# All score products of two attentions with 128 rows, in a fused kernel of two transformer blocks

## The chip, the cores and the metric

The kernel runs on one core of one Trainium2 chip, in one launch. The metric is its time on the device in microseconds; the median of several runs is given. A profile comes from one execution taken by the hardware profiler. The engines are named as the profile names them: PE (TensorE), PEld (its weight loads), DVE (VectorE), ACT (ScalarE), POOL (GpSimd) and SP (SyncE, which here issues most DMAs).

## The reference

Two blocks of two layers each, on 1024 tokens of 1024 features, all in float32. The first block has a dilated window attention (18 heads of 64 features in three groups with dilations 1, 4 and 16) and a latent attention. Each layer of the second block mixes tokens by a differential attention, a retention and a pooling, and then runs a convolutional MLP. The change concerns the scores of two of them:

```python
# dilated attention, one group: blocks of R queries against 3 R keys
s = jnp.einsum('bdhnqe,bdhnke->bdhnqk', qs, kb).astype(jnp.float32) * (Dh ** -0.5) + bias[:, None]
p = jnp.exp(s - m)
o = jnp.einsum('bdhnqk,bdhnke->bdhnqe', p, vb.astype(jnp.float32)) / denom
# differential attention: 4 heads, two maps m of 64 features each, causal
s = jnp.einsum('bhmqd,bhmkd->bhmqk', q_blk, k).astype(jnp.float32) * scale
p = jax.nn.softmax(jnp.where(mask, s, -jnp.inf), axis=-1)
a = p[:, :, 0] - lam * p[:, :, 1]
```

## The kernel before

A float32 matrix is kept as two float32r parts, a high part (the rounded value) and a low part (what is left), and a product is the sum of high times high, high times low and low times high. For scores over 64 features the kernel puts the high part of q in 64 of the 128 rows of a tile and the low part in the other 64. One product with 128 rows against k's high part, which stands in both halves, then gives (high + low of q) times high of k. A second product adds high of q times low of k; before the change it has 64 rows, because k's low part stands only in the half where q's high part is.

**Differential attention** (`diff_attention`, once per layer of the second block). Query tiles of 128 tokens are taken one after the other, 32 in all (four heads of eight). In step n, `scores(n, m)` computes the scores of both maps of tile n against its t + 1 key tiles (t = n % 8), so with 128 to 1024 columns, in pieces of at most 512, in two PSUM buffers `y`. A third product `dccm` adds the causal mask to the last 128 columns. VectorE takes the row maximum from PSUM (L1551), ScalarE the exponential (L1553), VectorE combines the two maps (L1559). `transpose(n - 2, ..)` and `values(n - 3)` follow two and three steps later, `project(n + 3)` computes q and k three tiles ahead, and `turn(n + 2)` transposes and splits them: k into `dk` (high) and `dkl` (low), tiles of a whole head with two buffers, q into `dq`. PE executes all this in the order of the program (`self.pin`).

**Dilated attention** (in `phase_A`). Nine groups are run through, three dilations g for each of three pairs of heads hp. `dil_batches` gives the score batches of a group; `step` lays the scores of a batch, the transposes and value products of the batch before, and pieces of the projection of the next group (`dil_project`, half projections of 24 products) between each other. The order of PE is the program's; a planner orders the other engines by the costs it assumes. `dil_project` evacuates q and k from PSUM (two buffers `g`) into their parts: `split_q` (L637, L639), `split_k` (L647, L649, L652). Group g = 2 keeps q and k in plain float32 (L631) and computes its scores in one product with 64 rows, which PE executes as two instructions. v goes through `vt` (L664) to be transposed. After the three groups of a head pair, `dil_weights` reads the row statistics back from DRAM, forms the weights of the groups and stores them (L835); `dil_product` loads them as `wb` (L528) and multiplies `sg` by them (L529).

**The raw ring.** `raw()` hands out five buffers of 128x1024 in turn. In the dilated attention weight columns come through it (`load_w`, L217, then split on DVE and POOL, L199 and L203), and the rows of `ada_w` of a background job, `mod_jobs` (L542, L552). SP issues DMAs in order, so one that waits for a buffer holds those behind it.

Of the kernel before, what the change touches and what calls it, by code (L numbers as in the profile page):

```python
# [12 lines left out]
F32 = mybir.dt.float32  # L13
F32R = mybir.dt.float32r
# [83 lines left out]
class UT:  # L98
    """Transposed activations, split in two float32r parts: [feature, token]."""
# [12 lines left out]
class Pools:  # L112
    """Several pools, chosen by tag."""
# [8 lines left out]
class TagPool:  # L122
    """One pool per tag (a new pool waits only for the pools it overlaps); a tile without a tag is a tag of its own."""
# [18 lines left out]
class Kern:  # L142
# [30 lines left out]
    def psum(self, ctx, left="", right=""):  # L173
        """One PSUM pool per tag, stacked from either end."""
        for side, tags in (("left", left), ("right", right)):
            for t in tags:
                self.ps.tags[t] = self.pool(ctx, "ps" + t, space=PSUM, side=side)

    def pp(self, tag, bufs, shape=None):
        """PSUM tile; a tag of a phase always comes with the same bufs."""  # L180
# [5 lines left out]
    def split(self, hi, lo, src, scale=None):  # L186
        """hi = float32r(src), lo = src - hi (src times scale), src in PSUM or SBUF."""
# [8 lines left out]
    def wsplit(self, hi, lo, raw, eng=None, cut=1, act=False):  # L196
        """Split, the high part on ScalarE if act; the low part in as many pieces as cut says (short ones delay other work
        of the engine less)."""
# [9 lines left out]
    def load_w(self, pool, w, c0, n, kts=KT, tag="w", bufs=None, dve=0, cut=1):  # L208
        """Weight columns c0..c0+n, split: w[kt][part] is [128, n]; every dve-th chunk on VectorE alone."""
# [15 lines left out]
    def next_w(self, c0, ahead=0):  # L225
        """The weight columns at c0 of the list in self.order, or those after them."""
# [7 lines left out]
    def gemm_T(self, w, ut, out, cols=slice(0, P)):  # L234
        """out [128 features, 1024 tokens] in PSUM, as two halves."""
# [10 lines left out]
    def gemm_N(self, ps, w, cols, lhs, kts=KT):  # L246
        """ps [128 tokens, features]; lhs(part, kt) is the stationary operand."""
# [7 lines left out]
    def transposes(self, dst, src, n):  # L255
        """dst [.., n, 128] = blocks of src [128, n * 128] transposed."""
# [3 lines left out]
    def to_T(self, src, ut, t):  # L260
        """src [128 tokens, 1024] in SBUF -> ut token tile t."""
# [6 lines left out]
    def rsqrt(self, y, v, pool, src=None, mul=1.0, eps=0.0):  # L268
        """y = v ** -0.5 (integer first guess, three Newton steps), v = src * mul + eps if src is given."""
# [20 lines left out]
    def silu2(self, out, src, tmp):  # L290
        """out = 2 silu(src) = src (1 + tanh(src / 2))."""
# [3 lines left out]
    def rms_rstd(self, src, n, eps, junk, pool):  # L295
        """[128, 1] = (mean(src ** 2) + eps) ** -0.5 over the free axis."""
# [13 lines left out]
    # ---------------------------------------------------------------- setup  # L310
# [11 lines left out]
    def transposed_columns(self, dst, rows_ap, nrow, pool):  # L322
        """dst [128, nrow] = rows_ap [nrow, 128] transposed."""
# [7 lines left out]
    # ---------------------------------------------------------------- first block, layer 0  # L331
    def phase_A(self, x_in):
        nc, i = self.nc, self.i
        with ExitStack() as ctx:
# [6 lines left out]
            with ExitStack() as c0:  # L341
# [23 lines left out]
                # relative position bias vectors, one row per head  # L365
# [11 lines left out]
                # shift and scale, one feature per partition  # L377
# [7 lines left out]
                # column c of block c: ones  # L385
# [69 lines left out]
            def fill(n):  # L455
                """PE work of the projections and gates, as many pieces."""
# [6 lines left out]
            def step(job, n):  # L463
                """The scores of job, with the rest of the one before it."""
# [42 lines left out]
    def dil_gate(self, lp, ut, w_in, hp, g, sgs):  # L507
        """2 silu(gate) of head pair hp of group g, transposed."""
# [13 lines left out]
    def dil_product(self, lp, hp, g, sgs, os, wtd, yT):  # L522
        """y^T rows of head pair hp of group g: attention times weight times gate."""
        nc = self.nc
        sg = sgs[hp, g]
        wb = lp.tile([P, S], F32, tag="wb", bufs=1, name=self.nm("wb"))
# [8 lines left out]
    def mod_jobs(self, lp, cs, jobs):  # L535
        """Thirds of silu(c) @ ada_w + ada_b of a layer, to DRAM, and the convolution taps by channel."""
# [63 lines left out]
    def dil_project(self, lp, ut, w_in, hp, g, res):  # L600
        """q, k, v of heads (2 hp, 2 hp + 1) of group g, tokens in the order of the group; v with tokens on
        partitions."""
# [24 lines left out]
        def tiles(*names):  # L627
            return [lp.tile([P, S], F32 if g == 2 else F32R, tag=n, bufs=2, name=self.nm(n)) for n in names]

        def plain(t, copy):  # L630
# [1287 lines left out]
```

## Time and profile before

| | before |
|---|---|
| median of 3 runs | 4187.02 us (4184.10 to 4189.52) |
| span of the profiled execution | 4168.8 us |
| PE busy | 3945.4 us, 95% |
| PE weight loads busy | 3282.7 us, 79% |
| VectorE busy | 2430.4 us, 58% |
| ScalarE busy | 1371.7 us, 33% |
| dilated attention | 77 to 637 us of the span |
| differential attentions | 1777 to 1993 us and 3077 to 3293 us |

The span runs from the first to the last instruction of the program; no other time of that execution is recorded, and the median of the runs lies 18.2 us above it. Matmuls are pipelined and the profile models their ends, so consecutive ones overlap in the rows; the distance from one start to the next is what a product takes of PE's time. In a row, `y<-dkl,dq 64*128 64x512` means: tile `y` is written from `dkl` (moving) and `dq` (stationary), 64 rows by 128 weight columns, 512 moving columns. What stands in brackets at the end is the idle time of the engine just before, and what ended it.

### The profile page before, as it was taken

How to read it: one execution, taken by the hardware profiler on the slowest of the kernel's cores; microseconds unless marked ns; L12 is line 12 of the kernel's file. 1: busy time of each engine (PE TensorE's matmuls, PEld its weight loads, DVE VectorE, ACT ScalarE, POOL GpSimd, SP SyncE). 2: the span in 40 equal slices, each digit the busy share in tenths (PEclk: the TensorE clock that was granted, in tenths of full speed). 3: DMA queues.
4: the chain of work that ended last, by engine and by line, in shares of the span. 5: the costliest groups of instructions: out<-in, count | busy, mean ns of one | idle time of the engine just before them, and what ended most of it. 6: DMA issues, size and time to landing. Idle time of an engine off the chain costs nothing. (4 is left out here: it accounts for less than half of the span.)

```text
span 4168.8 us, 54321 instructions
## 1 busy us (share of the span) xinstructions
PE 3945.4 (95%) x21085; PEld 3282.7 (79%) x21085; DVE 2430.4 (58%) x4606; ACT 1371.7 (33%) x2908; POOL 1087.9 (26%) x1016
## 2 busy tenths in 40 slices
PE   7989896899999889999999999997999999999998
PEld 5768775788888778988778888886988778888886
DVE  6545445947787767578753434438568764444436
ACT  3323331126777632255421111113235431111111
POOL 1111211410221322233133232324133222222233
PEclk9989998999999999999999999998999999999999
DMA  6363727320110243110421111113111231111112
GB/s 234 90 81 87 90 57 124 112 67 21 38 35 19 79 130 97 46 32 26 137 81 51 45 51 46 46 56 115 46 42 37 82 122 50 46 46 51 41 51 81
DMA packets 318896, 290.79 MB, mean 70 GB/s; under 512 B 70779, under 2 KB 273267, under 8 KB 318638
## 3 DMA queue, kind: packets, MB, share of 16 engines
q1 hardware_dynamic: 313362, 268.23, 23.8%
q10 hardware_dynamic: 5276, 19.08, 1.5%
q8 instruction: 167, 2.74, 0.3%
q14 instruction: 91, 0.75, 0.1%
HBM read 240.26 MB, written 51.72 MB: 70 GB/s over the span
## 5 line engine op out<-in xcount | busy, mean ns | idle before, releaser
L203 POOL TENSOR_TENSOR wl<-wr,wh 128x1024 fp32r<-128x1024 f32 (+1 forms) x253 | 497.9, 1977 | 1553.1 <-DVE wh L199 1458.8
L199 DVE CAST wh<-wr 128x1024 fp32r<-128x1024 f32 x222 | 180.2, 813 | 713.5 <-PE y L151 310.6
L151 PE MATMUL y<-uh_m,wl 128*128 128x512 f32 x1056 | 415.8, 394 | 4.7 <-DVE z L1643 4.2
L151 PE MATMUL y<-uh_m,wh 128*128 128x512 f32 x1056 | 418.6, 396 | 0.0
L151 PE MATMUL y<-ul_m,wh 128*128 128x512 f32 x1056 | 417.6, 395 | 0.0
L1796 ACT ACTIVATE cv<-y,cw 128x1024 f32<-128x1024 f32 x66 | 79.8, 1209 | 775.7 <-PE y L151 775.7
L151 PE MATMUL g<-uh_a,wl 128*128 128x512 f32 x568 | 234.8, 413 | 32.7 <-DVE sg L293 32.6
L151 PEld LDWEIGHTS y<-uh_m,wl 128*128 128x128 f32 x1056 | 198.2, 188 | 54.8 <-issue 4.6
L151 PEld LDWEIGHTS y<-uh_m,wh 128*128 128x128 f32 x1056 | 198.2, 188 | 48.2
L151 PEld LDWEIGHTS y<-ul_m,wh 128*128 128x128 f32 x1056 | 198.2, 188 | 47.5 <-DVE ul_m L191 0.9
L151 PE MATMUL g<-ul_a,wh 128*128 128x512 f32 x568 | 227.7, 401 | 0.5 <-POOL ul_a L422 0.4
L151 PE MATMUL g<-uh_a,wh 128*128 128x512 f32 x568 | 227.0, 400 | 0.0
L151 PE MATMUL y<-wo,yh 128*128 128x512 f32 x784 | 217.5, 400 | 2.7 <-ACT yh L1168 2.5
L191 DVE TENSOR_TENSOR pt<-t,pt 128x512 fp32r<-128x512 f32 x256 | 165.8, 680 | 21.9 <-ACT pt L190 21.0
L151 PEld LDWEIGHTS y<-wo,yh 128*128 128x128 f32 x784 | 147.7, 191 | 36.4 <-ACT yh L1168 4.3
L151 PE MATMUL y<-wl,hh 128*128 128x512 f32 x440 | 175.2, 398 | 0.0
L151 PE MATMUL y<-wh,hh 128*128 128x512 f32 x440 | 174.9, 398 | 0.0
L151 PE MATMUL y<-wh,hl 128*128 128x512 f32 x440 | 174.8, 397 | 0.0
L1005 DVE TENSOR_REDUCE nm<-s 128x1 f32<-128x1024 f32 x128 | 155.7, 1216 | 27.4 <-PE s L151 26.7
L151 PE MATMUL g<-wl,uh_n 128*128 128x256 f32 x576 | 166.2, 289 | 2.9 <-DVE dv L191 2.4
L151 PE MATMUL g<-wl,uh_f 128*128 128x256 f32 x576 | 166.0, 288 | 3.0 <-DVE dv L191 2.5
L151 PE MATMUL v<-pt,v 128*64 128x256 f32 (+1 forms) x1024 | 154.9, 294 | 10.2 <-DVE o L1040 10.2
(450 smaller groups left out, 10263.1 us busy)
## 6 DMA issues: line engine op xcount, KB each, us to landing
wr<-w_up SPq DMA_DIRECT2D x88, 512.0 KB
wr<-ada_w SPq DMA_DIRECT2D x48, 512.0 KB
wr<-w_down SPq DMA_DIRECT2D x44, 512.0 KB
wr<-a_w_in SPq DMA_DIRECT2D x36, 512.0 KB
wr<-w_in SPq DMA_DIRECT2D x24, 512.0 KB
xs<-wr SPq DMA_DIRECT2D x16, 512.0 KB
wr<-xs ACTq DMA_DIRECT2D x16, 512.0 KB
wr<-w_in SPq DMA_DIRECT2D x32, 256.0 KB
```

Source lines behind the costliest of these rows:

```text
L151: ins = self.nc.tensor.matmul(*args, **kw)
L191: nc.vector.tensor_tensor(lo, src, hi.bitcast(F32), OP.subtract)
L199: (self.nc.scalar.copy if act else self.nc.vector.tensor_copy)(hi, raw)
L203: (eng or self.nc.gpsimd).tensor_tensor(lo[..., cs], raw[..., cs], hi[..., cs].bitcast(F32), OP.subtract)
L1005: nc.vector.tensor_reduce(nm, sp, AX.X, OP.max, negate=True)
L1796: nc.scalar.activation(t, ps, AF.Identity, bias=cw[:, 3, c:c + 1], scale=cw[:, 2, c:c + 1])
```

## The change

The low part of k is written to both halves of the rows, so that the second score product can use all 128 rows of q as well: it gives (high + low of q) times low of k. This holds for the differential attention and for all three groups of the dilated one; group 2 loses its plain float32 path and gets the same two float32r products as the others. In the differential attention `dk` and `dkl` become tiles of 512 keys with three buffers, and one subtract of both maps replaces two. In the dilated attention `split_k` subtracts four times instead of two, into two tiles `kl0` and `kl1`. To make room, `vt`, `wb` and the tile of the statistics are taken from the raw ring instead of having buffers of their own. Docstrings and comments are removed throughout, which the diff below leaves out.

```diff
@@ dil_product, dil_weights
-        wb = lp.tile([P, S], F32, tag="wb", bufs=1, name=self.nm("wb"))
+        wb = self.raw()
@@ dil_project
         def tiles(*names):
-            return [lp.tile([P, S], F32 if g == 2 else F32R, tag=n, bufs=2, name=self.nm(n)) for n in names]
-
-        def plain(t, copy):
-            return lambda h, ps: copy(flat(t)[:, :, halves[h]], ps)
+            return [lp.tile([P, S], F32R, tag=n, bufs=2, name=self.nm(n)) for n in names]
...
         def split_k(k, low):
             def evac(h, ps):
                 for r, t in zip(rows, k):
                     nc.scalar.copy(flat(t[r])[:, :, halves[h]], ps[r])
-                for r, t in zip(rows, k):
-                    nc.vector.tensor_tensor(flat(low[r])[:, :, halves[h]], ps[r],
-                                            flat(t[r])[:, :, halves[h]].bitcast(F32), OP.subtract)
+                for r, o, t, u in zip(rows, rows[::-1], k, low):
+                    for d in (r, o):
+                        nc.vector.tensor_tensor(flat(u[d])[:, :, halves[h]], ps[r],
+                                                flat(t[r])[:, :, halves[h]].bitcast(F32), OP.subtract)
                 for r, o, t in zip(rows, rows[::-1], k):
                     nc.scalar.copy(flat(t[o])[:, :, halves[h]], ps[r])
...
-        if g == 2:
-            out += tiles("q0", "k0")
-            evacs = [plain(out[0], nc.scalar.copy), plain(out[1], nc.vector.tensor_copy)]
-        else:
-            q, k, low = tiles("q0", "q1"), tiles("k0", "k1"), tiles("kl")[0]
-            out += [q, (k, low)]
-            evacs = [split_q(q), split_k(k, low)]
-        vt = lp.tile([P, S], F32, tag="vt", bufs=1, name=self.nm("vt"))
+        q, k, low = tiles("q0", "q1"), tiles("k0", "k1"), tiles("kl0", "kl1")
+        out += [q, (k, low)]
+        evacs = [split_q(q), split_k(k, low)]
+        vt = self.raw()
@@ dil_batches, Job.scores
-                    if g == 2:
-                        kern.mm(sp[:rows, j, :], q[rs, q0:q0 + rows], k[rs, k0:k0 + wd], start=True, stop=True)
-                    else:
-                        qa, ka, low = q[hd.a][:, q0:q0 + rows], k[0][hd.a][:, k0:k0 + wd], k[1][rs, k0:k0 + wd]
-                        kern.mm(sp[:rows, j, :], qa, ka, start=True, stop=False)
-                        kern.mm(sp[:rows, j, :], qa[rs], low, start=False, stop=True)
+                    qa = q[hd.a][:, q0:q0 + rows]
+                    for n in range(2):
+                        kern.mm(sp[:rows, j, :], qa, k[n][hd.a][:, k0:k0 + wd], start=(n == 0), stop=(n == 1))
@@ diff_attention, turn
-            if t == 0:
-                ks[h] = (lp.tile([P, 2, S], F32R, tag="dk", bufs=2, name=self.nm("dk")),
-                         lp.tile([P, S], F32R, tag="dkl", bufs=2, name=self.nm("dkl")))
-            kk, kl = ks[h]
+            if t % 4 == 0:
+                ks[h, t // 4] = [lp.tile([P, 2, 512], F32R, tag=x, bufs=3, name=self.nm(x)) for x in ("dk", "dkl")]
+            kk, kl = ks[h, t // 4]
...
-            for m, r in enumerate(rows):
-                nc.vector.tensor_tensor(kl[r, ts], tp[r, 1 + m], kk[r, m, ts].bitcast(F32), OP.subtract)
+            nc.vector.tensor_tensor(kl[:, :, ts], tp[:, 1:3], kk[:, :, ts].bitcast(F32), OP.subtract)
@@ diff_attention, scores
-                self.mm(sp[:, cs], q[:, m], kk[:, m, cs], start=True, stop=False)
-                self.mm(sp[:, cs], q[r, m], kl[r, cs], start=False, stop=(c1 < W))
+                kk, kl = ks[h, c0 // 512]
+                self.mm(sp[:, cs], q[:, m], kk[:, m, :c1 - c0], start=True, stop=False)
+                self.mm(sp[:, cs], q[:, m], kl[:, m, :c1 - c0], start=False, stop=(c1 < W))
```

## Rows read from the trace of the kernel before

**Rows 1.** The page, busy time of each engine, share of the span, instructions.

```profile
PE 3945.4 (95%) x21085; PEld 3282.7 (79%) x21085; DVE 2430.4 (58%) x4606; ACT 1371.7 (33%) x2908; POOL 1087.9 (26%) x1016
```

**Rows 2.** Windows: stretch, length, busy us of PE, PEld, DVE, ACT, POOL, clock, DMA.

```profile
1776.80:1992.76 215.96, 214.55 (x1436) 177.81 (x1434) 172.77 (x485) 128.71 (x412) 74.52 (x213) 1.00 0.09 28
77.00:637.00 560.00, 522.54 (x2844) 417.00 (x2843) 265.41 (x406) 200.23 (x498) 95.29 (x38) 0.95 0.42 80
```

**Rows 3.** PE in order of time (start us, us, instruction): 512 columns, 256, 96 rows.

```profile
2299.61 0.39 PE L151 MATMUL y<-uh_m,wl 128*128 128x512 f32 x1
2299.84 0.39 PE L151 MATMUL y<-uh_m,wh 128*128 128x512 f32 x1
...
1843.95 0.28 PE L151 MATMUL g<-wh,ul_n 128*128 128x256 f32 x1
1844.07 0.28 PE L151 MATMUL g<-wl,uh_n 128*128 128x256 f32 x1
...
975.33 0.62 PE L151 MATMUL s<-kb,qh 96*128 96x512 f32 x2
```

**Rows 4.** PE in order of time in the differential attention, its scores, and four transposes.

```profile
1790.70 0.47 PE L151 MATMUL y<-dk,dq 128*128 128x512 f32 x1
1791.10 0.49 PE L151 MATMUL y<-dkl,dq 64*128 64x512 f32 x1
1791.52 0.33 PE L151 MATMUL y<-dccm 128*128 128x128 f32 x1
1791.68 0.39 PE L151 MATMUL g<-dv,dp 128*128 128x256 f32 x2
...
1987.85 0.60 PE L156 MATMUL t<-ident,de 128*128 128x128 f32 x4
...
3289.36 0.50 PE L151 MATMUL y<-dk,dq 128*128 128x512 f32 x1
```

**Rows 5.** PE in order of time in the dilated attention, scores of groups 0/1 and 2.

```profile
80.50 0.28 PE L151 MATMUL s<-k,q 128*128 128x256 f32 x1
...
599.30 0.38 PE L151 MATMUL s<-k,q 128*128 128x256 f32 x1
599.61 0.38 PE L151 MATMUL s<-kl,q 64*128 64x256 f32 x1
599.92 0.65 PE L156 MATMUL t<-ident,xs 128*128 128x128 f32 x4
...
205.69 0.22 PE L151 MATMUL o<-ptl,vh 128*64 128x128 f32 x1
205.84 1.16 PE L151 MATMUL s<-k,q 64*128 64x128 f32 x8
```

**Rows 6.** Groups of PE instructions by shape: count, busy us, mean ns, idle before.

```profile
L151 PE MATMUL y<-dk,dq 128*128 128x512 f32 x96 | 43.5, 453 | 0.9 <-ACT de L1553 0.9
L151 PE MATMUL s<-k,q 128*128 128x256 f32 x90 | 33.3, 370 | 0.0
```

**Rows 7.** Groups of DVE instructions in 1827 to 1884 us, by shape.

```profile
L1529 DVE TENSOR_TENSOR dkl<-t,dk 64x128 fp32r<-64x128 f32 x16 | 4.6, 285 | 0.7 <-ACT dq L1527 0.6
L191 DVE TENSOR_TENSOR dp<-t,dp 128x256 fp32r<-128x256 f32 x2 | 0.8, 412 | 0.0
```

**Rows 8.** Windows: last two tiles of a head, last three of the stage.

```profile
1867.42:1884.04 16.62, 16.62 (x106) 12.93 (x105) 14.70 (x42) 9.65 (x28) 3.53 (x15) 1.00 0.13 40
1973.71:1992.76 19.05, 17.64 (x91) 11.68 (x89) 18.42 (x46) 12.85 (x34) 7.17 (x14) 1.00 0.09 29
```

**Rows 9.** Groups of DVE instructions in 77 to 640 us, by shape.

```profile
L199 DVE CAST wh<-wr 128x1024 fp32r<-128x1024 f32 x32 | 22.1, 691 | 68.4 <-PE g L151 30.8 <-DMA wr<-a_w_in 19.8 <-issue 17.8
...
L649 DVE TENSOR_TENSOR kl<-g,k 64x512 fp32r<-64x512 f32 x20 | 13.8, 688 | 19.7 <-ACT k L647 19.5
```

**Rows 10.** DVE in order of time, a change of head pair.

```profile
277.48 1.22 DVE L529 TENSOR_TENSOR sg<-sg,wb 128x1024 f32<-128x1024 f32 x1 [15.34 <-DMA wb<-wtd]
```

**Rows 11.** SP's own waits in 77 to 640 us: us, times, longest.

```profile
SPq L217 <- POOL wl L203: 85.0, 14, 10.5
```

More of the change, by code (lines that the diff above doesn't have):

```diff
@@ L759, in scores @@
                 q, k = qkv[:2]
-                rs = slice(hd.r0, hd.r0 + 64)
                 nb = len(tl)
@@ L817, in dil_weights @@
         nc = self.nc
-        wb = lp.tile([P, S], F32, tag="wb", bufs=1, name=self.nm("st"))
+        wb = self.raw()
         st = wb[:, 0:96].rearrange("p (t a g s) -> p t a g s", t=NT, a=2, g=3)
@@ L1522, in turn @@
             self.transposes(tp, c.rearrange("p a b -> p (a b)"), 3)
-            ts = slice(t * P, (t + 1) * P)
+            ts = slice(t % 4 * P, (t % 4 + 1) * P)
             nc.scalar.copy(kk[:, :, ts], tp[:, 1:3])
@@ L1536, in scores @@
             W = (t + 1) * P
-            q, (kk, kl) = qs[n], ks[h]
+            q = qs[n]
             if m == 0:
@@ L1541, in scores @@
             es, sm, rs = ex[n]
-            r = slice(m * 64, (m + 1) * 64)
             sp = self.pp("y", 2, [P, 1024])
```

## The prediction, made before the result was known

> **What bounds the kernel now.** I read the page first [rows 1]: TensorE (PE) is busy in 95% of the span and VectorE in 58%, so PE is the engine to look at, but a mean over the span says nothing of one stage. The windows of the stages come next [rows 2]. In the differential attention of one layer (215.96 us; the second layer repeats it) PE is busy for 214.55 us, VectorE for 172.77 and ScalarE for 128.71, at a granted clock of 1.00. In the dilated attention (560 us) PE is busy for 522.54, VectorE for 265.41 and ScalarE for 200.23 us. PE bounds both stages, and in the differential one it shows no idle time.
>
> The third view is the order of time within PE, since a busy PE may be waiting inside itself. I read it from start to start, because the ends overlap. Where every product has 128 rows, one of 512 columns starts 0.23 us after the one before it, and one of 256 columns 0.12 us after [rows 3]. In the differential scores [rows 4] a product with 128 rows (`dk`) is followed by one with 64 (`dkl`). There 512 columns take 0.40 us until `dkl` starts and 0.42 until the next does, and even the small causal product behind it (`dccm`, 128 columns) holds its follower for 0.16 us. The dilated scores do the same: at 256 columns 0.31 us in and 0.31 out [rows 5]. The last rows of that group are the check inside the trace: in group 2 eight products of 64 rows stand (1.16 - 0.28)/7 = 0.13 us apart, but the first comes 0.15 us after the short product in front, which in [rows 3] proportion to its 128 columns should take 0.06. Products of 96 rows, which never change to 64, show nothing of it: two take 0.62 us together, so they start 0.23 apart [rows 3]. What costs is the passage between 64 and 128 rows, some 0.2 us each way; few rows as such cost nothing.
>
> **The change, differential attention.** No product is removed: the second gets 128 rows. Steps after the change come from [rows 3]: 0.231 us at 512 columns, 0.118 at 256, 0.174 at 384 (between them). At 128 columns the step is bounded below by half of that at 256, 0.06 us, and above by the transposes' (0.60 - 0.27)/3 = 0.11 [rows 4], which also bring 128 new weight columns each; I take 0.112, since these products bring as many. Steps before are means over all products of a shape, start to start; there are 96 of 512 columns [rows 6] and 32 of each other shape (for 512, the first at 1790.70 and the last at 3289.36 [rows 4]).
> 512 columns: 96 x (0.383 + 0.427 - 2 x 0.231) = 33.4 us.
> 384: 32 x (0.340 + 0.370 - 2 x 0.174) = 11.6. 256: 32 x (0.283 + 0.312 - 2 x 0.118) = 11.5. 128: 32 x (0.226 + 0.254 - 2 x 0.112) = 8.2.
> `dccm`: 128 x (0.164 - 0.112) = 6.7.
> Together 71.4 us for both layers, 35.7 each.
>
> The Trainium skill (TensorE: Matmul & The Clock Gate, section Back-to-back issue gap) gives about 131 ns for a product of 512 columns in a sustained stream. By it the new step would be 0.1 us shorter and the sum 192 x 0.1 = 19 us larger. The stream of this kernel stands at 0.23 us [rows 3], so the trace does not agree.
>
> How much of it reaches the end? PE then needs 216.0 - 35.7 = 180.3 us a layer. VectorE loses two subtracts of 64x128 per tile (0.285 us each) and gets one of 128x256, for which the `dp` subtract of that size stands, 0.41 us [rows 7]: 32 x 0.16 = 5 us less, so 167.7. PE still sets the mean pace, with VectorE loaded to 93%. The windows of single tiles [rows 8] show where that fails. In the two last tiles of a head VectorE is busy for 14.70 of 16.62 us; PE would need 16.62 - 3.1 = 13.5 us (eight pairs and four `dccm`), VectorE 14.4. It lacks 0.9 us a head, which the shorter tiles behind give back if it may lag; two score buffers in PSUM let it lag a little. I count half, over three heads: 1.5 us a layer. In the last three tiles of the stage VectorE is busy for 18.42 of 19.05 us already, while PE would save 5.0: nearly all of that is void, 4 us a layer. So 71.4 - 3 - 8 = 60 us. Ends: 71 us if VectorE always catches up, 42 if another quarter turns into waits on it.
>
> The finer tiles of `dk` and `dkl` (three halves of 512 keys for two whole heads) need the same space. A third buffer is written again two tiles after its last reader or later, so no wait is added. If one were, the tile's evacuation and with it PE would wait under 2 us, six times a layer.
>
> **The change, dilated attention.** Groups 0 and 1 have 90 pairs of 256 columns [rows 6] and 12 of 128. The steps of all 102 (first at 80.50, last at 599.30 [rows 5]), idle time left out, less 0.118 us for 256 columns and 0.060 for 128, come to 37.5 us. In group 2 each product was two passes in plain float32 and becomes two float32r products of 128 rows: as many instructions, 96, at 0.11 before and, by the bound for 128 columns, 0.11 after. Nothing, with ends of 5 us gained (0.06 a step) and 5 lost. Its twelve passages in and out of 64 rows go: 12 x (0.09 + 0.09) = 2.2 us. PE's part is 39.7 us.
>
> Against it stand longer evacuations. Groups 0 and 1 get 24 more subtracts of 64x512 on VectorE; group 2 gets 36 and loses 6 copies; at 0.69 us [rows 9] 54 x 0.69 = 37 us. ScalarE gets 36 casts for 6 copies, at no more than the same 0.69 each 21 us. Both engines are busy for under half of the 560 us [rows 2] and most of it lies beside PE's work. What can surface is the evacuation of k: two casts, four subtracts, two casts, 8 x 0.69 = 5.5 us at most (6 x before; one copy in group 2). Its PSUM buffer is wanted again after the next half projection, 24 x 0.23 = 5.5 us plus the attention work between. The cover is thin; without it some 1 us for each of 36 halves of q and k could show. I take 4 us.
>
> Part of the gain falls where PE is not late. At each change of head pair row statistics go to DRAM and back, and VectorE stands in front of `sg` times `wb` until a DMA lands, 15.34 us before 277.48 [rows 10]. Coming there earlier only lengthens that wait. The pairs between 240 and 280 and between 448 and 484 us carry 4.3 us of the gain: lost. So 39.7 - 4 - 4.3 = 31 us.
>
> **The ring.** `vt`, `wb` and the statistics move to the five buffers through which weights and ada rows come. SP waits there already: 85.0 us for POOL to finish `wl` [rows 11]. Behind such a wait everything else of SP's is queued: weights, bias tiles, statistics, `wb`, and VectorE waits for these. For the weights there is cover: VectorE's casts of them wait 30.8 us in all for PE to give up old ones [rows 9], so they come early. For ada rows and for the stretch after 637 us the sign is open: three `wb` can load without waiting for each other, but the statistics hold a buffer until their stores land. I take nothing, with ends of 10 us gained (the wait of 15.34 us shortened at one place) and 30 lost (two more of it).
>
> **Sum.** 60 + 31 = 91 us. The profiled span is 4168.8 us, 18.2 below the median of 4187.0; what lies around it is not touched. 4187 - 91 = 4096 us.
>
> **Rivals.**
> Forecast: the passages go and most of the time comes through, 4070 to 4140 us. Chance 0.82.
> VectorE sets the pace: its 43 us of idle a layer (215.96 - 172.77 [rows 2]) are bound to ScalarE and stay, so that only its 5 us less come through. 10 + 31 = 41 us: 4146. Against it: PE is never idle in [rows 2], so at present VectorE waits for PE. Chance 0.08.
> The passage isn't the cause: the second product costs 0.4 us for its other key tile, whatever its rows. Then only added work is left: 4187 to 4195, say 4190. Against it: products in [rows 3] change tiles too, at 0.23. Chance 0.04.
> Slower: the ring runs dry and SP's order does the rest. A group whose weights, ada rows and statistics stand in one line stalls PE by a stretch like 15.34 us [rows 10]; nine groups cost 138 us: 4187 - 91 + 138 = 4234. It decides from 91/9 = 10 us a group on. Against it: the weights come early [rows 9]. Chance 0.03.
> More: the dense step falls to 0.13 us, as the page named above has it. 192 steps shorten by 0.1 us: 4077. Chance 0.03.
>
> **How the numbers follow.** The likeliest is 4096 us. Low end: all of PE's gain (71 + 40 us) and a few us from the waits at the head pairs, 4070. High end: 42 us from the differential and 5 from the dilated attention, 4140. A measurement here tells some 0.2%, 8 us, from no change. Faster by more: 0.82 + 0.08 + 0.03 = 0.93; within: most of the third case, 0.03; slower: the fourth and what is left of the third, 0.04.
>
> **What would show it.** After the change `dk` to `dkl` at 512 columns must step by 0.23 us and `dccm` by 0.11. A differential stage must last 183 to 190 us with VectorE over 85% busy, and PE must wait for VectorE in its last three tiles. The dilated stage must last some 530 us, and PE's waits there must not grow by more than a few us even where SP's do. It is wrong if the steps stay at 0.4 us, or if PE's idle time in the dilated stage grows by over 15 us.

## The result, and the profile after

The changed kernel takes 4131.25 us (median of 4 runs, 4127.73 to 4135.21), the kernel before, on the same chip, 4185.83 (4 runs, 4184.10 to 4189.52). The ratio is 0.9863 with a 95% interval of 0.985 to 0.9877. The gain is 55 us; 91 were forecast. The time lies inside the range given, 35 us above the forecast. The profiled execution of the changed kernel took 4131.9 us, its span is 4130.1.

The page, busy time of each engine as in [rows 1]:

```profile
PE 3858.2 (93%) x21085; PEld 3272.8 (79%) x21085; DVE 2447.7 (59%) x4596; ACT 1382.1 (33%) x2938; POOL 1085.5 (26%) x1016
```

PE executes as many instructions as before and is busy for 87 us less (3945.4 - 3858.2), but the span is only 39 us shorter (4168.8 - 4130.1). So most of what was forecast did leave PE, and more than half of it came back as idle time. The windows of the two stages, columns as in [rows 2], tell where:

```profile
1788.70:1978.60 189.90, 182.13 (x1435) 173.49 (x1433) 165.93 (x453) 125.81 (x412) 75.33 (x213) 1.00 0.10 32
77.00:638.60 561.60, 489.36 (x2845) 405.46 (x2844) 292.73 (x453) 216.26 (x529) 92.99 (x37) 0.94 0.40 75
```

The differential stage of one layer fell from 215.96 to 189.90 us. The dilated stage did not move (560.00 before, 561.60 after), although PE is busy there for 33 us less: PE's time without work rose from 37.5 to 72.2 us. The order of time within PE, as in [rows 4] and [rows 5], first the differential and then the dilated scores:

```profile
1872.96 0.39 PE L151 MATMUL y<-dkl,dq 128*128 128x512 f32 x1
1873.19 0.39 PE L151 MATMUL y<-dk,dq 128*128 128x512 f32 x1
1873.42 0.40 PE L151 MATMUL y<-dkl,dq 128*128 128x512 f32 x1
1873.66 0.22 PE L151 MATMUL y<-dccm 128*128 128x128 f32 x1
1873.72 0.96 PE L151 MATMUL g<-dv,dp 128*128 128x256 f32 x7
...
580.69 0.28 PE L151 MATMUL s<-kl,q 128*128 128x256 f32 x1
580.80 0.28 PE L151 MATMUL s<-k,q 128*128 128x256 f32 x1
...
209.34 0.27 PE L151 MATMUL s<-kl,q 128*128 128x128 f32 x1
209.45 0.28 PE L151 MATMUL s<-k,q 128*128 128x128 f32 x1
```

The instructions are as long as before; their starts have moved together. At 512 columns the step is 0.23 us in place of 0.40 and 0.42, at 256 columns 0.11 to 0.12 in place of 0.31. The causal product `dccm` lets its follower start after 0.06 us (0.16 before). The two-product scores of group 2 step by 0.11, as the two passes in plain float32 did. Not every start comes so close: over the whole differential stage the step behind `dccm` is 0.085 us in the mean, and that behind `dk` at 512 columns 0.273, since those that follow a transpose take 0.32 (they start 0.03 us behind it, where a transpose in a row of transposes holds the next for 0.11).

What PE waited for in the dilated stage (line waited for: us in total, times, longest), in the kernel before:

```profile
PE o L151 <- DVE ptl L191: 14.4, 4, 9.6
PE t L156 <- DVE vl L191: 7.3, 3, 3.0
PE g L151 <- DVE sg L293: 7.2, 1, 7.2
```

and in the changed one, with a line of VectorE's own waits below:

```profile
PE g L151 <- DVE sg L293: 33.5, 2, 18.7
PE t L156 <- DVE vl L191: 21.2, 6, 7.8
...
DVE wh L199 <- DMA wr<-a_w_in: 95.1, 13, 27.5
```

The last line is the one to compare with [rows 9]: VectorE's casts of the weights waited 19.8 us for the fetch then, and 95.1 now; their waits for PE fell from 30.8 to 9.4. The weights used to be early in most places and now are late in most. How that stops PE is seen in the order of time at the first change of head pair. SP issues:

```profile
236.88 11.72 SPq L825 DMA_DIRECT2D wtd<-wr  x6
248.64 5.25 SPq L528 DMA_DIRECT2D wr<-wtd  x2
253.93 0.67 SPq L217 DMA_DIRECT2D wr<-a_w_in  x1
```

and VectorE, in the same stretch (start us, us, instruction, idle time in front of it and what ended it):

```profile
273.93 0.69 DVE L199 CAST wh<-wr 128x1024 fp32r<-128x1024 f32 x1 [23.55 <-DMA wr<-a_w_in]
274.54 0.68 DVE L293 SCALAR_TENSOR_TENSOR sg<-th,g 128x512 f32<-128x512 f32 x1
```

In the kernel before the same weight fetch went out ahead of the six stores of the group weights (`wtd`):

```profile
227.88 0.38 SPq L217 DMA_DIRECT2D wr<-a_w_in  x1
...
243.20 10.38 SPq L835 DMA_DIRECT2D wtd<-st  x6
```

Now its buffer of the ring is free only later, so it stands behind these stores and lands after 20 us. VectorE works in order and stands in front of the cast for 23.55 us; behind the cast is `sg`, which empties a PSUM buffer `g` that PE wants. PE stands still for 14.8 us:

```profile
260.06 0.39 PE L151 MATMUL g<-ul_a,wh 128*128 128x512 f32 x1
275.28 0.79 PE L151 MATMUL g<-uh_a,wl 128*128 128x512 f32 x1 [14.82 <-DVE sg L293]
275.87 0.63 PE L151 MATMUL g<-uh_a,wh 128*128 128x512 f32 x1
276.29 0.63 PE L151 MATMUL g<-ul_a,wh 128*128 128x512 f32 x1
```

At the next change of head pair it stands still for 18.7 us, and there the stores act in another way. SP's issues, and below them its own wait (us, times, longest):

```profile
469.03 1.34 SPq L542 DMA_DIRECT2D wr<-ada_w  x1
484.79 0.38 SPq L217 DMA_DIRECT2D wr<-a_w_in  x1
...
SPq L217 <- DMA wtd<-wr: 14.3, 1, 14.3
```

Here the fetch is not even issued before 484.79 us. It gets the place of the ring that holds the statistics, and SP waits until the last of the six stores that read from this place has landed, 32 us after the first was issued (452.67). The fetch itself then takes 5 us to the cast behind it.

### The profile page after: what moved, and what is told of

It is laid out like the page before. It is cut to its first block, busy times and chain, and to the rows that moved or that the text cites. A ratio compares the mean times of both kernels' runs of the same rounds, so it can differ in the third digit from the quotient of the medians.

```text
span 4130.1 us, 54373 instructions
## 1 busy us (share of the span) xinstructions
PE 3858.2 (93%) x21085; PEld 3272.8 (79%) x21085; DVE 2447.7 (59%) x4596; ACT 1382.1 (33%) x2938; POOL 1085.5 (26%) x1016
## 5 line engine op out<-in xcount | busy, mean ns | idle before, releaser
L151 PEld LDWEIGHTS y<-wo,yh 128*128 128x128 f32 x784 | 149.2, 193 | 50.7 <-ACT yh L1158 18.5
L151 PEld LDWEIGHTS g<-uh_a,wl 128*128 128x128 f32 x568 | 111.5, 196 | 78.9 <-DVE sg L293 49.5
```

The lines of the kernel that those rows point to most:

```text
L151: ins = self.nc.tensor.matmul(*args, **kw)
```

## The experiments

Three explanations for the missing part were put to the test. A: the ring makes the weights late, and PE's waits at the changes of head pair take what the scores gave. B: the longer evacuations (VectorE busy for 292.73 us in place of 265.41 [rows 2]) hold PE up. C: the trip of the row statistics through DRAM sets the time at those places, whatever PE gains. Ratios are those to the kernel before on the same chip, with 95% intervals. 4 us are 0.1%.

**e0_before**, the kernel before, unchanged, to have a second profile of it.

> The kernel before, profiled again on the chip of these runs. The profile that the prediction used had a span of 4168.8 us, 15 us less than the other executions took. All theories: some 4185 us; the 15 us should then lie in the stages with DMA round trips (the dilated attention and what follows it, 77 to 840 us) and none in the differential attention, whose stage is bound by PE and should last 216 us in this profile too.

Measured: 4191.34 us, once; the span is 4189.6, 20.8 us more than that of the profile on which the prediction rests. PE's idle time in the dilated stage is 41.4 us (37.5 there). Most of the difference stands in the differential stages (217.9 us from the first to the last `dk` product in place of 212.2, in both layers). The expectation had none of it there, so it missed; the last section shows what differs.

**e1_diff**, the differential part of the change alone, on the kernel before:

```diff
@@ diff_attention
+                ks[h, t // 4] = [lp.tile([P, 2, 512], F32R, tag=x, bufs=3, name=self.nm(x)) for x in ("dk", "dkl")]
...
+            nc.vector.tensor_tensor(kl[:, :, ts], tp[:, 1:3], kk[:, :, ts].bitcast(F32), OP.subtract)
...
+                self.mm(sp[:, cs], q[:, m], kl[:, m, :c1 - c0], start=False, stop=(c1 < W))
```

> Only the differential attention has the second score product with 128 rows; the dilated attention is as before. If the two parts don't touch each other: the two stages last 190 us instead of 216, 52 us less, 4134 us, which is all of the change's gain. If the forecast's 31 us from the dilated attention were real and something in the differential part had eaten it instead: 4160 us or more.

Measured: 4127.07 us, ratio 0.9868 (0.9854 to 0.9883). That is the gain of the whole change, 56 us.

**e2_dil**, the rest of the change alone, on the kernel before (two products with 128 rows in all groups, two `kl`, the ring):

```diff
@@ dil_project, dil_batches, dil_product, dil_weights
+        q, k, low = tiles("q0", "q1"), tiles("k0", "k1"), tiles("kl0", "kl1")
...
+                        kern.mm(sp[:rows, j, :], qa, k[n][hd.a][:, k0:k0 + wd], start=(n == 0), stop=(n == 1))
...
+        vt = self.raw()
...
+        wb = self.raw()
```

> Only the dilated attention is changed (128-row products, longer evacuations, the three tiles in the raw ring); the differential attention is as before. Theory: its gain of 40 us of PE time is eaten by waits of its own, so 4183 us, within 8 us of before. If the dilated part gains what was forecast: 4155 us.

Measured: 4179.70 us, ratio 0.9999 (0.9987 to 1.0012). The dilated part is worth nothing (between 5 us gained and 5 lost), though its scores take 39.7 us in place of 73.7 (all 300 products, start to start, idle time left out). PE's idle time rose to 70.7 us. The two parts are additive: 0.9868 times 0.9999 is 0.9867, the change 0.9863.

**e3_ring**, the ring alone:

```diff
-        wb = lp.tile([P, S], F32, tag="wb", bufs=1, name=self.nm("wb"))
+        wb = self.raw()
...
-        vt = lp.tile([P, S], F32, tag="vt", bufs=1, name=self.nm("vt"))
+        vt = self.raw()
...
-        wb = lp.tile([P, S], F32, tag="wb", bufs=1, name=self.nm("st"))
+        wb = self.raw()
```

> The kernel before with nothing changed but the ring: vt, wb and the tile of the statistics come from the raw ring; scores and evacuations as before. Theory A (the ring makes weights late): slower by 20 to 40 us, 4205 to 4225 us, and VectorE's casts of weights wait for their DMA for far more than the 19.8 us of before. Theory B (the longer evacuations of q and k eat the gain): no change, 4185 us. Theory C (PE arrives earlier but the statistics' trip through DRAM sets the time of the stage anyway): no change, 4185 us.

Measured: 4198.54 us, ratio 1.0034 (1.002 to 1.0048), 14 us slower (8 to 20), less than the 20 to 40 that A had named. Its waits in the dilated stage, PE's and below them VectorE's:

```profile
PE g L151 <- DVE sg L293: 31.9, 2, 17.7
...
DVE wh L199 <- DMA wr<-a_w_in: 89.1, 11, 27.6
```

These two are the changed kernel's waits, without any change to a product or an evacuation. The late weights come from the ring.

**e4_vt**, of the ring only `vt`:

```diff
-        vt = lp.tile([P, S], F32, tag="vt", bufs=1, name=self.nm("vt"))
+        vt = self.raw()
```

> The kernel before with vt alone in the raw ring; wb and the tile of the statistics keep their own buffer. With all three in the ring the kernel was 14 us slower (4198.5), of which some 9 us came after the last value product of the dilated attention, where no vt is alive. If the ring hurts by the places that vt holds while weights should be fetched: some 4 to 10 us slower, 4187 to 4193. If wb and the statistics do it all: no change, 4183.

Measured: 4180.70 us, ratio 1.0017 (1.0005 to 1.0029): 7 us slower, half of the ring's cost at a first estimate, with an interval of 2 to 12 us.

**e5_work**, the kernel before with the evacuations of the changed one (in groups 0 and 1 every subtract of k is made twice; in group 2 `evac_q` makes two casts and two subtracts, `evac_k` two casts, four subtracts and two casts; what they add is never read):

```diff
+                    for _ in range(2):
+                        nc.vector.tensor_tensor(flat(low[r])[:, :, halves[h]], ps[r],
+                                                flat(t[r])[:, :, halves[h]].bitcast(F32), OP.subtract)
...
-            evacs = [plain(out[0], nc.scalar.copy), plain(out[1], nc.vector.tensor_copy)]
+            evacs = [evac_q, evac_k]
```

> The kernel before with the evacuations of the kernel after and nothing else of it: the 24 extra subtracts of groups 0 and 1 write the same values a second time, and group 2 gets the six subtracts and casts for each half, into tiles that nobody reads; scores, ring and buffers as before. Theory B (longer evacuations make PE wait): slower by 12 to 17 us, 4195 to 4200. Theory C (the statistics' trip through DRAM sets the time) and theory A (the ring): no change, 4183.

Measured: 4181.82 us, ratio 1.0024 (1.0015 to 1.0034), 10 us slower. B had named 12 to 17. The profile can't place them: its execution was the shortest of the ten, 4174.48 us, 7 under their median. In it PE is idle for 42.6 us in the dilated stage (41.4 in e0_before), and the stage is as long as before (561.8 us). That the evacuations cost about 10 us is measured; where they do is not shown.

**e6_rows**, 128 rows without ring and without further evacuations, by reading the high part of k twice (it leaves out the low part's share of the scores):

```diff
-                        kern.mm(sp[:rows, j, :], qa[rs], low, start=False, stop=True)
+                        kern.mm(sp[:rows, j, :], qa, ka, start=False, stop=True)
```

> The kernel before with the second score product of groups 0 and 1 at 128 rows and neither ring nor evacuation of the kernel after: it takes the high part of k again instead of the low part, so that the low part's share of the scores is left out and the high part's is counted twice. Theories A and B (the rows bring PE's time, ring and evacuation eat it): 34 us of PE less 4 at the changes of head pair, 4153. Theory C: PE's gain turns into waits even so, less than 10 us comes through, 4173 or more.

Measured: 4146.62 us, ratio 0.994 (0.992 to 0.9959), 25 us faster (17 to 33). The rows of groups 0 and 1 are worth this much where nothing else is changed; the score time fell to 42.0 us. With the ring's 14 and the evacuations' 10 us the sum is 1 us, and e2_dil shows 0. A and B together close the account; that A is the larger of the two isn't clear of the noise (8 to 20 us against 6 to 14).

**e7_g2plain**, the changed kernel, but group 2 as before:

```diff
-        q, k, low = tiles("q0", "q1"), tiles("k0", "k1"), tiles("kl0", "kl1")
+        if g == 2:
+            out += tiles("q0", "k0")
+            evacs = [plain(out[0], nc.scalar.copy), plain(out[1], nc.vector.tensor_copy)]
...
```

> The kernel after (4131 us) with group 2 of the dilated attention as before: plain float32, one product of 64 rows, short evacuations; that takes 30 of the 54 added VectorE operations and all 30 of ScalarE's away and brings its twelve passages back. Theory B: faster than after by 5 to 10 us, 4121 to 4126. Theories A and C: the passages cost 2 us and nothing else changes, 4133.

Measured: 4113.49 us, ratio 0.9862 (0.9845 to 0.9878), against 0.9863 for the change as a whole. By the ratio group 2 plays no part. By the trace PE's idle time in the dilated stage is 61.3 us, 11 less than in the changed kernel, and the median is 14 to 18 us below the changed kernel's on other chips; on this chip the kernel before was 6 to 12 us quicker than on those too (4173.86). The changed kernel wasn't run on this chip, so group 2's share stays open.

The next four were run on one chip, where the kernel before took 4180.36 us. Theory A had by then a sharper form: it isn't the ring's lateness by itself, but that a weight fetch which the ring delays falls behind the six stores of `wtd`, which write single elements of 4 bytes.

**e9_after**, the changed kernel again.

> The changed kernel again, to stand beside the three others on the same chip: ratio 0.986, TensorE idle from 77 us to the last values about 72 us.

Measured: 4127.49 us, ratio 0.9872 (0.9858 to 0.9885), idle time 72.1 us.

**e11_store**, the changed kernel with the group weights transposed on PE, so that one store of 48 rows of 512 bytes replaces the six:

```diff
-        for g in range(3):
-            for a in range(2):
-                nc.sync.dma_start(wtd[hp, g, a, :].rearrange("(t p) -> p t", p=P), z[:, :, a, g])
...
+        def store():
+            ps = self.pp("t", 2)
+            self.tr(ps[:48, :P], wb[:, 176:224], self.ident)
+            zt = lp.tile([P, 512], F32, tag="xs", bufs=3, name=self.nm("zt"))[:48, :P]
+            nc.vector.tensor_copy(zt, ps[:48, :P])
+            nc.sync.dma_start(wtd[hp].rearrange("g a (t p) -> (g a t) p", p=P), zt)
```

> The changed kernel, but the weights of the dilated product go to DRAM by one transpose on TensorE and one store of contiguous 512-byte rows, in place of six stores of single elements, three times in the dilated stage. Theory A (the weights of the next head pair are late because they stand behind these stores in SP's queue): TensorE idle from 77 us to the last values falls from 72 to 45 to 62 us, VectorE's wait of the cast wh on the fetch of a_w_in from 95 us to under 60, ratio 0.980 to 0.984. Rival (the weights are late because the ring's places come free late, whatever stands in the queue): idle 68 to 76 us, ratio 0.985 to 0.988, and the weights are issued as late as before.

Measured: 4068.47 us, ratio 0.9727 (0.9714 to 0.9741), 59 us faster than the changed kernel and more than theory A had expected, in the ratio and in the idle time, which fell to 36.3 us; VectorE's casts wait 50.7 us for the fetches in place of 95.1. The edit also puts the store behind the transpose and so later, at 253.45 us, where the six went out from 236.88 on. SP's issues at the same change of head pair, and VectorE's cast of the weights:

```profile
253.45 0.34 SPq L837 DMA_DIRECT2D wtd<-zt  x1
254.91 1.26 SPq L535 DMA_DIRECT2D wr<-wtd  x2
256.27 0.54 SPq L217 DMA_DIRECT2D wr<-a_w_in  x1
...
263.90 0.72 DVE L199 CAST wh<-wr 128x1024 fp32r<-128x1024 f32 x1 [1.77 <-DMA wr<-a_w_in]
```

Here the weights are issued as late as before (256.27 us, 253.93 in the changed kernel), as the rival said. They land after 7.6 us in place of 20. At the next change they are issued at 450.85 us, 2.6 us behind the store, in place of 484.79, 32 behind the first of the six: there the place in the ring is free as soon as the one store has landed. So the rival has the issue time right in one place of two, and the price wrong in both: a fetch that is issued late costs PE next to nothing, unless it meets those stores, on the engines or in the ring. C as it was put falls too: the statistics still go to DRAM and back here, and PE's waits for `sg` are gone. What the stores do is seen in the DMA lines of a stretch of 40 us (40 slices: busy tenths of the 16 DMA engines, GB/s moved; then packets, among them those under 512 B). In the changed kernel, from 230 us on:

```profile
DMA  9406000178796999999999899999999599962369
GB/s 320 56 0 45 4 0 0 1 6 2 1 1 0 0 1 0 1 2 2 1 0 0 0 1 9 13 5 17 29 25 25 20 41 45 70 66 27 66 216 214
DMA packets 9336, 1.33 MB, mean 33 GB/s; under 512 B 7860, under 2 KB 9200, under 8 KB 9335
```

and with the one store, from 250 us on:

```profile
DMA  0000107958999219895986698758982000790000
GB/s 0 0 0 0 41 0 209 197 159 208 333 171 219 66 53 406 197 373 201 279 143 205 266 332 202 153 86 209 376 345 94 8 0 9 215 295 6 0 0 0
DMA packets 5608, 6.06 MB, mean 151 GB/s; under 512 B 1330, under 2 KB 4578, under 8 KB 5604
```

In the first the 16 engines are full from about 238 to 265 us; they move 0 to 2 GB/s for most of it. The changed kernel again, packets from 238 to 258 and from 259 to 266 us:

```profile
DMA packets 5756, 0.06 MB, mean 3 GB/s; under 512 B 5746, under 2 KB 5746, under 8 KB 5756
...
DMA packets 164, 0.29 MB, mean 42 GB/s; under 512 B 49, under 2 KB 99, under 8 KB 164
```

For the first 20 us 24 KB of weights (six stores of 4 KB) in 4-byte packets keep the engines busy, and the weight column of 512 KB issued at 253.93 meets them. Behind them the engines stay full with the loads of the rows just stored (`wr<-wtd`), which were issued ahead of the fetch: a 4 KB packet of these takes 1.4 to 4.5 us there, against some 0.3 in e11_store. Why they are slow behind such stores isn't shown. The Trainium skill (DMA: Bandwidth & Descriptors, section Rules for kernel authors) says that an access whose last dimension isn't contiguous becomes one descriptor per element; six stores of 1024 elements would be 6144, an estimate. The trace agrees: 6530 fewer packets under 512 B in these two stretches, which aren't quite the same work.

38 of the gained 63 us of the span (4125.5 in e9_after, 4062.1) lie in the dilated stage, 19 in the stretch behind it up to the first product of the output weights (46.2 to 27.4 us), where the third set of stores stands.

**e8_single**, e1_diff and of the dilated part only the rows, without ring and evacuations:

```diff
-                        qa, ka, low = q[hd.a][:, q0:q0 + rows], k[0][hd.a][:, k0:k0 + wd], k[1][rs, k0:k0 + wd]
+                        qa, ka, low = q[hd.a][:, q0:q0 + rows], k[0][hd.a][:, k0:k0 + wd], k[1][:, k0:k0 + wd]
...
-                        kern.mm(sp[:rows, j, :], qa[rs], low, start=False, stop=True)
+                        kern.mm(sp[:rows, j, :], qa, low, start=False, stop=True)
```

> The differential part of the change, and of the dilated part only the rows: the second score product of groups 0 and 1 takes all 128 rows of q against the single tile of low parts (the other 64 rows add low(q) times the other head's low(k), which is of the size of the term that the split drops anyway). No raw ring, no longer evacuation, own buffers as in the kernel before. Theory A plus B (the rows are worth 25 us, and the ring and the evacuations ate them): the gains of the differential part alone (0.9868) and of the rows alone (0.994) add up, ratio 0.979 to 0.983, 70 to 88 us faster than the kernel before and 15 to 30 faster than the changed kernel; TensorE idle from 77 us to the last values about 43 us, score time there about 42. Theory that the rows' gain is lost anyway once the differential part is there (something outside sets the end): 0.986 as the changed kernel.

Measured: 4098.97 us, ratio 0.9801 (0.9787 to 0.9814): 81 us faster than the kernel before, 28.5 faster than the changed one. The gains of the two parts add up (0.9868 times 0.994 is 0.9809); the product with 128 rows needs neither the second `kl` nor its buffers.

**e12_both**, e8_single with the one store.

> Single-tile rows without the ring, together with the contiguous store. Theory A says that without the ring the weights are already early, so that the store is worth little here: ratio 0 to 0.002 below that of the single-tile kernel without it (0.977 to 0.983). If the store's queue time itself delays the product and the tail: 0.003 or more below it.

Measured: 4050.43 us, ratio 0.9686 (0.9673 to 0.97), the fastest of all: 130 us under the kernel before, 77 under the changed one. The store is worth 48.5 us even without the ring, so the first expectation, that it is worth little there, failed, and the second held more strongly than it said. The kernel before had the stalls too, in another place: the wait of 15.34 us for `wb` in [rows 10] was one of these. Its load went out at 272.67 us, 0.2 us after the last of the six stores had landed; PE stood still for 9.6 us behind it (the wait for `ptl` in the list above), and for 7.2 at the next change, where a fetch issued behind the stores took 20 us. In e8_single these two are 12.3 and 9.2 us, in e12_both they are gone. The windows of the dilated stage, e11_store and e12_both:

```profile
77.00:595.60 518.60, 482.33 (x2846) 400.34 (x2844) 289.56 (x455) 215.93 (x529) 93.79 (x37) 0.97 0.30 81
...
77.00:585.90 508.90, 482.75 (x2844) 400.88 (x2843) 263.09 (x408) 199.46 (x498) 95.09 (x38) 0.98 0.32 89
```

PE's idle time is 36.3 and 26.2 us. What the ring, the evacuations and group 2's products cost together when the stores are out of the way is the difference of the two kernels, 18 us. Part of it shows: PE waits 20.7 us for `vl` in e11_store and 10.2 in e12_both.

## Why the prediction was right, and where it was not

**The passage between 64 and 128 rows** was the right cause. Steps of 0.23 us at 512 columns were forecast and measured. `dccm` went to 0.085 us in the mean (0.06 where PE's stream is dense) where 0.112 was taken. Over one differential stage the score products and `dccm` take 42.7 us in place of 77.9, start to start without idle time: 35.2 us of gain, 35.7 forecast. That the sum fits so closely is in part luck: in both layers the pairs of 512 columns gave 29 us of the 33.4 counted, because a `dk` behind a transpose still takes 0.32 us, and `dccm` gave 10 of 6.7.

**What VectorE gives back there** was mis-sized. The prediction counted 5.5 us a layer. The two last tiles of a head take 14.67 us (14.4 forecast from VectorE), and in the last three tiles of the stage almost nothing is gained, as forecast (0.85 us; PE's saving there was put at 5.0, but the sum's own steps make it 4.5, and 3.0 in place of 3.1 for the two tiles):

```profile
1866.23:1880.90 14.67, 13.84 (x107) 12.91 (x105) 14.11 (x40) 9.65 (x28) 5.49 (x19) 1.00 0.11 36
1960.70:1978.90 18.20, 14.34 (x91) 11.68 (x89) 18.00 (x46) 12.29 (x34) 7.91 (x14) 1.00 0.12 39
```

These answer [rows 8]: 16.62 and 19.05 us before. PE's idle time rose by 6.4 us (1.4 to 7.8), 0.9 more than counted. Another 2.8 us went into the transposes and value products, whose steps became longer by as much in sum. Some 2 us of it stand at the twelve waits for `dp`: the row in front of such a wait ends, as the profile models ends, some 0.16 us after its follower would have started, and so much of the wait isn't shown as idle time. The rest stays open. 35.2 - 6.4 - 2.8 = 26.0 us a layer, 52 in both, where 60 were forecast. VectorE is busy for 165.93 us, 87% of the stage (167.7 forecast), and PE waits for it in the last tiles. The stage of 189.9 us lies at the upper end of the 183 to 190 named.

**The dilated part** was forecast at 31 us and is worth 0. The gain of PE was 33 us in the changed kernel (73.3 to 40.1) where 39.7 were taken; the steps at 256 columns came to 0.154 us behind `k` and 0.143 behind `kl` in the mean, not 0.118. Of it, the test named in the prediction says what became: wrong, if PE's idle time there grows by over 15 us. It grew by 34.8.

The step that failed is the one on the ring: "I take nothing", because the casts of the weights waited 30.8 us for PE in all [rows 9], "so they come early". That is a sum over the stage. The wait beside it, in the kernel before (us in total, times, longest):

```profile
DVE wh L199 <- DMA wr<-a_w_in: 19.8, 2, 17.1
```

One fetch was late by 17.1 us, so they did not come early everywhere; and [rows 10] showed a DMA landing late at just such a place. The prediction saw SP's order as the danger, but asked only who waits for a free buffer, not what the fetch would then be queued behind. It even said that the statistics hold a buffer of the ring until their stores land, and priced it at nothing. What the runs showed in its place: the ring alone costs 14 us (e3_ring), because the fetches then meet stores that take some 30 us to land. The prediction's rival (the ring runs dry and SP's order does the rest, 9 stalls of 15.34 us) named the mechanism; there were two such stalls of PE, of 14.8 and 18.7 us, not nine. The bound of 30 us for the ring's cost held. Of the 31 us that are missing the ring has 14 and the evacuations 6 (10 for 4); the rows of groups 0 and 1 brought 25 us (e6_rows) where 37.5 less the 4.3 of the head pairs had been counted, 8 us less. Each of these is uncertain by some 5 us or more.

**The evacuations**: VectorE has 27 us more to do (37 forecast), ScalarE 16 (21 forecast). 4 us were taken as surfacing; e5_work has 10 (6 to 14).

**Group 2**: its 96 score instructions took 13.1 us and take 11.3, 1.8 us less where 2.2 were taken for the passages; its share by its evacuations stays open (e7_g2plain).

**The base of the sum** had a flaw. The profiled execution was 18.2 us below the median, and the prediction took what lies between as untouched. Between that profile and the one of e0_before, which is 20.8 us longer, 11.4 us of the difference stand in the differential stages, where the change works (last section). A gain of 52 us by the profile and of 56 (49 to 61) by the runs of e1_diff fit each other.

## What to carry to other kernels

Moving a buffer into a shared ring changes the order of a DMA queue, so look up, for each transfer that gets later, which transfers it then stands behind, which hold the place that it gets, and what these cost the DMA engines, before taking the mean of its slack as cover. Where a product's step is longer than that of products of the same size, look at the rows that it and its neighbours use; a missing half whose product is negligible needs no exact copy (e8_single). When a stage doesn't shorten although its engine works less, find the wait that took the place: here it was older than the change, and removing it was worth 59 us with the ring and 48.5 without it.

## What the runs showed of the hardware

**The passage between 128 and 64 rows.** In the differential scores `dkl` at 512 columns stepped by 0.427 us in the mean with 64 rows and steps by 0.232 with 128, with the same columns and as many products. A `dk` right behind it stepped by 0.429 and steps by 0.230; one behind a projection product by 0.325 and by 0.230. This last difference, 0.09 us, is the same at 128 and 256 columns (0.150 to 0.058, 0.210 to 0.117).

**4-byte stores.** 24 KB in single elements, three times in this kernel, took 25 to 32 us from the first of the six issues to the last landing; one store of 48 rows of 512 bytes took 1.4 to 4.1. A 512 KB fetch issued meanwhile took 20 us to the start of the cast behind it, in place of 7.6.

**The clock after a standstill.** Windows of 270 to 275, 275 to 290 and 290 to 295 us of the changed kernel, the granted clock being the number after POOL's:

```profile
270.00:275.00 5.00, 0.00 (x0) 0.00 (x0) 1.07 (x2) 0.00 (x0) 0.30 (x1) 0.50 0.60 142
275.00:290.00 15.00, 14.27 (x70) 10.52 (x71) 10.86 (x15) 4.44 (x12) 6.30 (x3) 0.80 0.37 116
290.00:295.00 5.00, 5.00 (x24) 4.11 (x23) 1.38 (x2) 0.65 (x3) 2.74 (x2) 1.00 0.97 245
```

While PE stood still the granted clock fell to 0.50 (1.2 GHz), and it was back at 1.00 (2.4 GHz) only some way into the work behind. The first products of 512 columns behind the stall start 0.42 us apart (275.87 and 276.29 above), where 0.23 is the step at 1.00 (1872.96 and 1873.19). So a stall costs more than its own length. The two kernels in sum: PE is busy for 489.4 us in the dilated stage of the changed kernel and for 482.3 in that of e11_store, with one product or transpose more. How much of these 7 us is the clock isn't worked out here.

**The same stage in two lengths.** In the kernel before, the last tiles of the differential attention ran at either level of the clock. From e0_before, and below it the same stretch of work from the profile of before and from the changed kernel:

```profile
1985.00:1990.00 5.00, 4.56 (x18) 3.32 (x17) 4.91 (x10) 2.87 (x10) 2.53 (x3) 0.70 0.00 0
1990.00:1995.00 5.00, 5.00 (x16) 3.03 (x14) 4.03 (x12) 2.78 (x8) 0.00 (x0) 0.50 0.00 0
1995.00:2000.00 5.00, 5.00 (x17) 3.69 (x18) 2.13 (x5) 1.35 (x4) 0.00 (x0) 0.50 0.00 0
```

```profile
1978.40:1983.40 5.00, 4.53 (x22) 2.75 (x20) 4.91 (x10) 3.38 (x11) 2.48 (x3) 1.00 0.00 0
1983.40:1988.40 5.00, 5.00 (x28) 3.50 (x28) 4.97 (x15) 3.48 (x9) 0.00 (x0) 1.00 0.00 0
```

```profile
1965.00:1970.00 5.00, 4.49 (x28) 3.73 (x29) 4.89 (x10) 3.28 (x12) 3.82 (x5) 1.00 0.00 0
```

In e0_before the clock falls to 0.50 where PE's stream thins out, for some 14 us, and the stage is 5.7 us longer. In the profile of before the same stretch ran at 1.00. Among the seven profiles of the kernel before and of the variants that keep its differential attention, the long stage stands in both layers of one (e0_before), in one layer of two (e3_ring, e4_vt) and in none of four: 4 of 14 stages. The seven profiles with the changed attention show it at 186.1 to 186.5 us from the first to the last `dk` product in all 14. So the change may also have taken away a part of the spread, up to 11 us in an execution, which a single profile of before could not show; 14 stages don't prove it. Why the clock falls there in one execution and not in the next isn't settled.
